# A gated two-branch layer: 128x128 transposes moved from TensorE to VectorE's square blocks and DMA

## The chip, the cores and the metric

The kernel runs on one core of one Trainium2 chip. The metric is the device time of one execution in microseconds (us). Of the kernel before, three runs were timed: 711.83, 712.28 and 712.83 us, median 712.28. One further execution was profiled; every duration below comes from it.

## The reference

One layer on x of 512 tokens and 1024 channels, in float32. A normalised x is projected to many columns at once; two token mixers take their parts, and their outputs are gated, projected and merged.

```
h    = rmsnorm(x) ;  proj = h @ w_in + b_in
mq, mk, mv, mi, mf, mo, mz, sq, sk, sv, sz, gates = split(proj)
# A) 4 memory heads of 256: causal conv and silu on mq, mk; chunkwise mLSTM with decay weights
hm   = rmsnorm(mlstm(mq, mk, mv, mi, mf))       per head
y_m  = hm * sigmoid(mo) * silu(mz)
# B) 8 attention heads of 128, "stick breaking", strictly causal
z    = (rmsnorm(q) @ rmsnorm(k).T) * scale
a    = sigmoid(z) * product over the keys between of (1 - sigmoid(z))
y_s  = (a @ v) * silu(sz)
out  = x + (sigmoid(g_m) * (y_m @ w_proj_m) + sigmoid(g_s) * (y_s @ w_proj_s)) @ w_out
```

## The kernel before, in words

**Precision.** A float32 product is made of three matmuls in a reduced format: each operand is split into a high part (ScalarE copies and rounds, L90) and a low part (VectorE subtracts, L91), and `mm3` (L85 to L87) adds high by high, high by low and low by high.

**Units.** The dense work is a list of 118 units, each with one 512 KB tile of weights. A unit is 24 matmuls of 512 columns in two halves. `chan_group` makes units whose result has channels on the partitions (one unit per 128 channels); `tok_group` makes units whose result has tokens on the partitions (four units for 512 channels, results all evicted at the end of the fourth). Units 0 to 31 are q, k, V and z (the gate) of attention set 0 and set 1, four heads in each; 32 to 71 belong to the two pairs of memory heads; 72 to 87 are the merge gates; then come the projections and the output.

**The main loop.** For each unit c the loop evicts the result of unit c-1, splits the weights of unit c+2 (AHEAD), issues the load of unit c+4 (LOADS), issues the unit's first half on TensorE, resumes every active head once, and issues the unit's second half. The heads are generators: at each `yield` a head stops until the next unit. So a head's small matmuls stand between dense matmuls, and a head takes as many units as it has yields. A head begins at or after its number in SB_START or M_START; in the units in REST no head is resumed. All engines work their instructions in the order in which the loop issued them. SyncE issues the loads in that order too, and it stands still at one whose buffer is not free or whose semaphore is still in use.

**An attention head** (`SbSet.head`). First step: q and k of the head are transposed on TensorE (L389) and split. Second: scores of query blocks 3, 0 and 1 on TensorE; `weigh` makes the weights of blocks 3 and 0 out of them (two sigmoids on ScalarE at L414 and L418, masks on GpSimd, a scan over the products at L422 and a product at L423 on VectorE). Third: the same for blocks 1 and 2. Now a_t[i], a part of the tile a_all (tag A, four buffers), holds weights with queries on the partitions; the product with V needs keys there. `turn` transposes the 128x128 blocks on TensorE by the identity (L447), into PSUM, and splits the result out of PSUM into at_split (tag P5, two buffers). `turn((0,))` and `turn((1,))` take 4 + 3 blocks in the fourth step, `turn((2, 3))` 2 + 1 blocks in the fifth, ten in all; `apply` multiplies with V in the fifth and sixth, and at L475 VectorE multiplies the gate y_s by the result. The fourth step waits until V of the set is complete.

**A memory head** (`MPair.head`). Row by row of key blocks `score` makes p_all (high and low, tag A); `num(i)` makes the output of token block i, VectorE and ScalarE normalise it into hns (L752, L755; tag P5). After the last one, eight 128x128 blocks are transposed on TensorE (L769) into PSUM, and VectorE multiplies y_m by them (L771).

Of the kernel before, what the change touches and what calls it, by code (L numbers as in the profile page):

```python
# [23 lines left out]

SB_START = [10, 13, 16, 20, 27, 30, 33, 36]
M_START = [52, 56, 70, 76]
GATES_PREP, GATES_START = 3, 4
REST = {11, 16, 20, 23, 24, 28, 44, 64}  # L30
AHEAD, LOADS = 2, 4


# [1 line left out]
def tile_hybrid_layer(  # L35
# [16 lines left out]
    nc = tc.nc  # L52
# [8 lines left out]
    sp = pool("sp")  # L61
# [19 lines left out]
    def att_ps():  # L81
        return psa.tile([128, 512], F32, name="aps", tag="aps")
# [6 lines left out]
    def split(src, hi, lo):  # L89
        nc.scalar.activation(hi, src, AF.Copy)  # L90
        nc.vector.tensor_tensor(lo, src, hi.bitcast(F32), op=OP.subtract)  # L91
# [119 lines left out]
    ident = cst.tile([128, 128], F32, name="ident")  # L211
# [97 lines left out]
    y_m = [None] * 8  # L309
    done = set()  # L310

    class SbSet:
# [70 lines left out]
        def head(self, h):  # L383
            hs = slice(h * 128, (h + 1) * 128)
            tr = []
            for name in ("q", "k"):
                tp = att_ps()
                for tb in range(TB):
                    nc.tensor.transpose(tp[:, tb * 128:(tb + 1) * 128], self.raw[name][tb][:, hs], ident)  # L389
                th = blk("qk", FR, name=name + "th")  # L390
                tl = blk("qk", FR, name=name + "tl")
                if name == "q":
                    nc.scalar.activation(th, tp, AF.Copy, scale=qkw)
                    nc.vector.scalar_tensor_tensor(tl, tp, qkw, th.bitcast(F32), op0=OP.mult, op1=OP.subtract)
                else:
                    split(tp, th, tl)
                tr.append((th, tl))
            yield
            (qh, ql), (kh, kl) = tr
            a_all = sp.tile([128, 1280], F32, name="a_all", tag="A", bufs=4)  # L400
            a_t = [a_all[:, 64 * i * (i + 1):64 * (i + 1) * (i + 2)] for i in range(TB)]

            def score(i, zp):
                n = (i + 1) * 128
                ts = slice(i * 128, n)
                mm3(zp, qh[:, ts], ql[:, ts], kh[:, 0:n], kl[:, 0:n], True, True)

            def weigh(i, zp):
                n = (i + 1) * 128
                ts = slice(i * 128, n)  # L410
                r, rn = self.r[i]
                om = blk("om", shape=(516,))
                be = a_t[i]
# [8 lines left out]
                nc.vector.tensor_tensor_scan(back, back, back, 1.0, op0=OP.mult, op1=OP.bypass)  # L422
                nc.vector.tensor_tensor(be, be, om[:, 1:n + 1], op=OP.mult)  # L423
# [7 lines left out]
            yield  # L431
            z2 = att_ps()
            score(2, z2[:, 0:384])
            weigh(1, z01[:, 128:384])
            weigh(2, z2[:, 0:384])
            yield
            while not ("v", self.s) in done:
                yield
            a_parts = {}

            def turn(js):
                tp = att_ps()
                at = 0
                for j in js:
                    n = T - j * 128
                    for i in range(j, TB):
                        nc.tensor.transpose(tp[:, at + (i - j) * 128:at + (i - j + 1) * 128],  # L447
                                            a_t[i][:, j * 128:(j + 1) * 128], ident)
                    at += n
                ap = blk("P5", FR, (2, 512), name="at_split")  # L450
                ah, al = ap[:, 0, :], ap[:, 1, :]
                split(tp[:, 0:at], ah[:, 0:at], al[:, 0:at])
                at = 0
                for j in js:
                    n = T - j * 128
                    a_parts[j] = ah[:, at:at + n], al[:, at:at + n]
                    at += n
# [140 lines left out]
    class MPair:  # L598
# [84 lines left out]
        def head(self, h):  # L683
            hd = 2 * self.p + h
# [50 lines left out]
            def num(i):  # L735
# [18 lines left out]
                nc.gpsimd.tensor_tensor(r, r, dn, op=OP.mult)  # L754
                return lambda: nc.scalar.activation(hn, sum_v, AF.Copy, scale=r)  # L755

            scale = [num(0), num(1)]
            for i in (2, 3):
                yield
                for fn in scale:  # L760
                    fn()
                scale = [num(i)]
            yield
            scale[0]()
            yield
            for d in range(2):
                tp = att_ps()
                for i in range(TB):
                    nc.tensor.transpose(tp[:, i * 128:(i + 1) * 128], hns[:, i, d * 128:(d + 1) * 128], ident)  # L769
                y = y_m[2 * hd + d]  # L770
                nc.vector.tensor_tensor(y, tp, y, op=OP.mult)  # L771


    sets = [SbSet(0), SbSet(1)]
# [4 lines left out]
    sets[0].z_group()  # L779
    sets[1].qk_group("q", C_SQ)  # L780
    sets[1].qk_group("k", C_SK)
    sets[1].v_group()
    sets[1].z_group()
    for p in pairs:
        p.o_group()
        p.z_group()
# [426 lines left out]
```

## Time and profile before

| | |
|---|---|
| median of three runs | 712.28 us (711.83 to 712.83) |
| profiled execution, its own time | 712.63 us |
| its span on the core | 710.9 us |
| TensorE busy | 702.3 us, 3332 matmuls |
| VectorE busy | 446.6 us, 711 instructions |
| ScalarE busy | 335.6 us, 629 instructions |
| GpSimd busy | 107.6 us, 249 instructions |
| mean granted TensorE clock | 0.999 |
| bytes moved by DMA | 73.57 MB, mean 103 GB/s |

The difference of 1.7 us between the execution's time and its span lies before the first and after the last instruction. In the profile PE is TensorE's matmuls, PEld its weight loads, DVE VectorE, ACT ScalarE, POOL GpSimd, SP SyncE; a q behind an engine's name stands for its sequencer, which waits and issues DMAs. L447 is line 447 of the kernel. A group's row ends in "busy us, mean ns | idle time before, and what ended it". A tile's name stands without its number, so that wl<-stg,wh reads: the low half wl is written from stg and wh. Matmuls overlap: a record of 390 ns for a 512-column matmul does not mean that they follow each other at that distance.

### The profile page before, as it was taken

To read this page: it belongs to the slowest core of one execution; us is meant where nothing else is said; L and a number is where in the kernel's file an instruction comes from. 1 tells how busy PE (TensorE), PEld (TensorE's weight loads), DVE (VectorE), ACT (ScalarE), POOL (GpSimd) and SP (SyncE) were. 2 spreads that over 40 slices of the span, in tenths; PEclk is the share of its full clock that TensorE was granted. 3 is DMA by queue.
4 is the path that set the end of the run, shared out by engine and by line. 5 is a ranking of instruction groups with operands and counts; after the bars stand their busy time and mean duration, and the time that the engine had idled before them with its cause. 6 is when DMAs were issued, how large, how long until landed. Compare 5 with 4: busy or idle time off the path is not lost.

```text
span 710.9 us, 9127 instructions
## 1 busy us (share of the span) xinstructions
PE 702.3 (99%) x3332; PEld 587.3 (83%) x3332; DVE 446.6 (63%) x711; ACT 335.6 (47%) x629; POOL 107.6 (15%) x249
## 2 busy tenths in 40 slices
PE   7999999999999999999999999999999999999997
PEld 5888888888888888888888888888888888888876
DVE  6837886656487567379954637885433244535896
ACT  6245364376355445144465634447464353334461
POOL 5412022253012112000011110000111000011010
PEclk9999999999999999999999999999999999999999
DMA  6433322232323223333332233333322236489434
GB/s 242 134 105 87 106 83 81 63 102 73 104 77 90 59 60 89 103 90 89 89 89 89 59 105 89 89 89 89 89 60 66 84 119 221 138 191 206 133 78 130
DMA packets 93492, 73.57 MB, mean 103 GB/s; under 512 B 3694, under 2 KB 77832, under 8 KB 93448
## 3 DMA queue, kind: packets, MB, share of 16 engines
q1 hardware_dynamic: 91288, 67.10, 32.6%
q0 software_dynamic: 2016, 5.77, 4.4%
q8 instruction: 26, 0.43, 0.2%
q14 instruction: 18, 0.15, 0.1%
q10 hardware_dynamic: 144, 0.13, 0.1%
HBM read 65.12 MB, written 2.10 MB: 95 GB/s over the span
## 4 chain that ended last, share of the span: by engine, by line
PE 97%; DMA 1%; DVE 1%; POOL 0%; SPq 0%; issue 0%; ACT 0%; DVEq 0%
PE dps L85 27%; PE dps L86 27%; PE dps L87 27%; PE aps L86 3%; PE aps L87 3%; PE aps L85 3%; PE aps L447 1%; PE aps L389 1%; PE dps L1102 1%; PE dps L1100 1%; PE dps L1101 1%; DMA stg<-in_w_in_dram 1%; PE aps L742 1%; PE aps L744 1%; PE aps L743 1%; PE aps L769 0%
## 5 line engine op out<-in xcount | busy, mean ns | idle before, releaser
L91 DVE TENSOR_TENSOR wl<-stg,wh 128x1024 fp32r<-128x1024 f32 x92 | 112.7, 1225 | 123.7 <-ACT wh L90 123.5
L85 PE MATMUL dps<-hh,wh 128*128 128x512 f32 x448 | 175.5, 392 | 0.0
L87 PE MATMUL dps<-hh,wl 128*128 128x512 f32 x448 | 174.8, 390 | 0.0
L86 PE MATMUL dps<-hl,wh 128*128 128x512 f32 x448 | 174.7, 390 | 0.0
L90 ACT ACTIVATE wh<-stg 128x1024 fp32r<-128x1024 f32 x92 | 96.8, 1052 | 63.3 <-PE dps L87 41.2
L87 PEld LDWEIGHTS dps<-hh,wl 128*128 128x128 f32 x448 | 84.2, 188 | 17.6
L85 PEld LDWEIGHTS dps<-hh,wh 128*128 128x128 f32 x448 | 84.2, 188 | 16.7
L86 PEld LDWEIGHTS dps<-hl,wh 128*128 128x128 f32 x448 | 84.2, 188 | 16.7
L85 PE MATMUL dps<-wh,hh 128*128 128x512 f32 x224 | 88.3, 394 | 0.0
L87 PE MATMUL dps<-wh,hl 128*128 128x512 f32 x224 | 87.4, 390 | 0.0
L86 PE MATMUL dps<-wl,hh 128*128 128x512 f32 x224 | 87.4, 390 | 0.0
L87 PEld LDWEIGHTS dps<-wh,hl 128*128 128x128 f32 x224 | 42.1, 188 | 8.9
L85 PEld LDWEIGHTS dps<-wh,hh 128*128 128x128 f32 x224 | 42.1, 188 | 8.2
L86 PEld LDWEIGHTS dps<-wl,hh 128*128 128x128 f32 x224 | 42.1, 188 | 8.2
L633 DVE SCALAR_TENSOR_TENSOR acc<-tmp,vec,acc 128x511 f32<-128x511 f32 (+2 forms) x48 | 36.0, 750 | 1.7
L636 ACT ACTIVATE tmp<-acc 128x512 f32<-128x512 f32 x16 | 10.1, 634 | 50.2 <-DVE acc L633 50.2
L416 POOL TENSOR_SCALAR_AFFINE_SELECT om<-om 128x128 f32<-128x128 f32 x32 | 12.1, 379 | 134.5 <-ACT om L414 134.5
L422 DVE TENSOR_TENSOR_SCAN om<-om 128x512 f32<-128x512 f32 (+3 forms) x32 | 27.9, 872 | 6.3 <-POOL om L416 6.3
L695 POOL TENSOR_SCALAR_AFFINE_SELECT w_all<-om 128x128 f32<-128x128 f32 x16 | 5.1, 355 | 167.1 <-DVE om L690 167.1
L90 ACT ACTIVATE at_split<-aps 128x384 fp32r<-128x384 f32 (+1 forms) x24 | 11.8, 525 | 36.8 <-PE aps L447 36.8
L91 DVE TENSOR_TENSOR at_split<-aps,at_split 128x384 fp32r<-128x384 f32 (+1 forms) x24 | 13.7, 599 | 19.8 <-ACT at_split L90 19.8
L85 PE MATMUL dps<-yh,wh 128*128 128x512 f32 x64 | 24.9, 389 | 0.0
(273 smaller groups left out, 1249.5 us busy)
## 6 DMA issues: line engine op xcount, KB each, us to landing
stg<-in_w_in_dram SPq DMA_DIRECT2D x87, 512.0 KB, 3.6
stg<-in_w_proj_s_dram SPq DMA_DIRECT2D x8, 512.0 KB, 4.0
B<-in_w_out_dram SPq DMA_DIRECT2D x8, 512.0 KB, 5.1
stg<-in_w_proj_m_dram SPq DMA_DIRECT2D x8, 512.0 KB, 3.6
wl<-stg POOLq DMA_DIRECT2D x8, 512.0 KB, 5.6
brow<-in_b_in_dram SPq DMA_DIRECT2D x8, 256.0 KB, 3.8
xr<-in_x_dram SPq DMA_DIRECT2D x8, 256.0 KB, 7.1
out_dram<-xr SPq DMA_DIRECT2D x7, 256.0 KB, 2.0
```

Of the source, the lines that this page charges most:

```text
L85: nc.tensor.matmul(ps, ah, bh, start=first, stop=False)
L86: nc.tensor.matmul(ps, ah, bl, start=False, stop=False)
L87: nc.tensor.matmul(ps, al, bh, start=False, stop=last)
L90: nc.scalar.activation(hi, src, AF.Copy)
L91: nc.vector.tensor_tensor(lo, src, hi.bitcast(F32), op=OP.subtract)
L389: nc.tensor.transpose(tp[:, tb * 128:(tb + 1) * 128], self.raw[name][tb][:, hs], ident)
L416: nc.gpsimd.affine_select(out=om[:, ts], in_=om[:, ts], compare_op=OP.is_gt, fill=1.0, base=0, channel_multiplier=1, pattern=[[-1, 128]])
L422: nc.vector.tensor_tensor_scan(back, back, back, 1.0, op0=OP.mult, op1=OP.bypass)
L447: nc.tensor.transpose(tp[:, at + (i - j) * 128:at + (i - j + 1) * 128], a_t[i][:, j * 128:(j + 1) * 128], ident)
L633: nc.vector.scalar_tensor_tensor(acc[:, j:], t[:, 0:T - j], cw(3 - j, ch), acc[:, j:], op0=OP.mult, op1=OP.add)
L636: nc.scalar.activation(t, acc, AF.Sigmoid)
L742: nc.tensor.matmul(nm[:, 0:258], ph, vh, start=j == 0, stop=False)
```

## The change

The transposes of L447 and L769 leave TensorE. VectorE's transpose turns each 32x32 square of a tile in its place, so that within each square rows and columns are exchanged, while the squares stay where they are. The exchange of the squares across partitions is made by DMAs from SBUF to SBUF, each of 32 partitions.

- Attention heads: `blocks(i)` turns the i+1 blocks of 128x128 of a_t[i] into a new tile ay (tag A, like a_all). Blocks 3 and 0 are turned in the third step, ahead of `weigh(1)` and `weigh(2)`; blocks 1 and 2 in a new step of their own. Then sixteen DMAs on SyncE's queue fill az (tag P5), eight in a step and eight in the next; one more step passes; then `turn` splits az, in SBUF, into ath and atl (tag y). A head has four more steps, and three fewer PSUM tiles.
- Memory heads: `turn(i)` turns hns of token block i into ht (tag A); turn(0) and turn(1) are issued ahead of num(3), turn(2) and turn(3) one and two steps later. Sixteen DMAs fill hz (tag A) in one step, and two steps later VectorE multiplies y_m by hz. A head has three more steps.
- SB_START begins the heads 3, 4, 5, 6 and 7 one, one, two, two and two units earlier; in REST 28 becomes 32; set 1's gate z comes ahead of its V.

```diff
-SB_START = [10, 13, 16, 20, 27, 30, 33, 36]
+SB_START = [10, 13, 16, 19, 26, 28, 31, 34]
-REST = {11, 16, 20, 23, 24, 28, 44, 64}
+REST = {11, 16, 20, 23, 24, 32, 44, 64}
...
+            ay = sp.tile([128, 4, 10, 32], F32, name="ay", tag="A", bufs=4)
+
+            def blocks(i):
+                for j in range(i + 1):
+                    nc.vector.transpose(ay[:, :, slot[i, j], :],
+                                        a_t[i][:, j * 128:(j + 1) * 128].rearrange("p (a j) -> p a j", j=32))
+
             z2 = att_ps()
             score(2, z2[:, 0:384])
+            blocks(3)
+            blocks(0)
             weigh(1, z01[:, 128:384])
             weigh(2, z2[:, 0:384])
+            yield
+            for i in (1, 2):
+                blocks(i)
+            yield
+            az = sp.tile([128, 4, 10, 32], F32, name="az", tag="P5", bufs=2)
+            for b in range(4):
+                for a in range(4):
+                    nc.sync.dma_start(az[32 * a:32 * a + 32, b, :, :], ay[32 * b:32 * b + 32, a, :, :])
+                if b == 1:
+                    yield
+            yield
             yield
             while not ("v", self.s) in done:
                 yield
...
             def turn(js):
-                tp = att_ps()
...
-                        nc.tensor.transpose(tp[:, at + (i - j) * 128:at + (i - j + 1) * 128],
-                                            a_t[i][:, j * 128:(j + 1) * 128], ident)
...
-                split(tp[:, 0:at], ah[:, 0:at], al[:, 0:at])
...
+                ah, al = blk("y", FR, name="ath"), blk("y", FR, name="atl")
+                split(az[:, :, n0:n1, :].rearrange("p b i j -> p i b j"),
+                      *[x[:, 0:at].rearrange("p (i b j) -> p i b j", b=4, j=32) for x in (ah, al)])
...
+            ht = sp.tile([128, 8, TB, 32], F32, name="ht", tag="A", bufs=4)
+
+            def turn(i):
+                nc.vector.transpose(ht[:, :, i, :], hns[:, i, :].rearrange("p (x j) -> p x j", j=32))
+
             scale = [num(0), num(1)]
             for i in (2, 3):
                 yield
                 for fn in scale:
                     fn()
+                if i == 3:
+                    turn(0)
+                    turn(1)
                 scale = [num(i)]
             yield
             scale[0]()
+            turn(2)
+            yield
+            turn(3)
+            yield
+            hz = sp.tile([128, 2, T], F32, name="hz", tag="A", bufs=4)
+            src = ht.rearrange("p (d a) i j -> p a d (i j)", d=2)
+            for a in range(4):
+                for b in range(4):
+                    nc.sync.dma_start(hz[32 * a:32 * a + 32, :, 128 * b:128 * b + 128],
+                                      src[32 * b:32 * b + 32, a])
+            yield
             yield
             for d in range(2):
-                tp = att_ps()
-                for i in range(TB):
-                    nc.tensor.transpose(tp[:, i * 128:(i + 1) * 128], hns[:, i, d * 128:(d + 1) * 128], ident)
-                y = y_m[2 * hd + d]
-                nc.vector.tensor_tensor(y, tp, y, op=OP.mult)
+                y = y_m[2 * hd + d].rearrange("p (i b j) -> p i b j", i=TB, b=4)
+                z = hz[:, d, :].rearrange("p (b i j) -> p i b j", i=TB, b=4)
+                nc.vector.tensor_tensor(y, z, y, op=OP.mult)
...
     sets[1].qk_group("k", C_SK)
+    sets[1].z_group()
     sets[1].v_group()
-    sets[1].z_group()
```

How the change moves instructions is shown at three places, in the order in which they stand on an engine, first before and then after. The first is TensorE in a unit in which one head applies its first weights and another computes scores (dps is dense work, aps a head's; at_split, then ath and atl, are the split weights, vh and vl V, kth and qth the split k and q). Before:

```order
L87 MATMUL dps<-hh,wl 128x512
L85 MATMUL aps<-at_split,vh 128x512
L86 MATMUL aps<-at_split,vh 128x512
L87 MATMUL aps<-at_split,vl 128x512
L85 MATMUL aps<-at_split,vh 128x384
L86 MATMUL aps<-at_split,vh 128x384
L87 MATMUL aps<-at_split,vl 128x384
L447 MATMUL aps<-ident,a_all 128x128 x3
L85 MATMUL aps<-kth,qth 128x384
L86 MATMUL aps<-ktl,qth 128x384
L87 MATMUL aps<-kth,qtl 128x384
```

After:

```order
L87 MATMUL dps<-wh,hl 128x512
L85 MATMUL aps<-ath,vh 128x512
L86 MATMUL aps<-atl,vh 128x512
L87 MATMUL aps<-ath,vl 128x512
L85 MATMUL aps<-ath,vh 128x384
L86 MATMUL aps<-atl,vh 128x384
L87 MATMUL aps<-ath,vl 128x384
L85 MATMUL aps<-kth,qth 128x512
L86 MATMUL aps<-ktl,qth 128x512
```

The product with V is followed at once by the scores of another head (here blocks 3, 0 and 1 instead of block 2, since the heads now stand otherwise to each other); no L447 stands between, there or anywhere else.

The second place is VectorE in the units 13 to 15, with heads 0 and 1 (SCALAR_TENSOR_TENSOR at L422 is the scan, wl the low half of weights two units ahead). Before:

```order
L325 SCALAR_TENSOR_TENSOR ys<-dps,bvec,tmp 128x512
L91 TENSOR_TENSOR wl<-stg,wh 128x1024
L422 SCALAR_TENSOR_TENSOR om<-om 128x256
L423 TENSOR_TENSOR a_all<-a_all,om 128x256
L422 SCALAR_TENSOR_TENSOR om<-om 128x384
L423 TENSOR_TENSOR a_all<-a_all,om 128x384
L394 SCALAR_TENSOR_TENSOR qtl<-aps,qkw,qth 128x512
L91 TENSOR_TENSOR ktl<-aps,kth 128x512
L325 SCALAR_TENSOR_TENSOR ys<-dps,bvec,tmp 128x512
L91 TENSOR_TENSOR wl<-stg,wh 128x1024
L91 TENSOR_TENSOR at_split<-aps,at_split 128x512
L91 TENSOR_TENSOR at_split<-aps,at_split 128x384
```

After:

```order
L91 TENSOR_TENSOR wl<-stg,wh 128x1024
L440 STREAM_TRANSPOSE ay<-a_all 128x4x32 x5
L422 SCALAR_TENSOR_TENSOR om<-om 128x256
L423 TENSOR_TENSOR a_all<-a_all,om 128x256
L422 SCALAR_TENSOR_TENSOR om<-om 128x384
L423 TENSOR_TENSOR a_all<-a_all,om 128x384
L394 SCALAR_TENSOR_TENSOR qtl<-aps,qkw,qth 128x512
L91 TENSOR_TENSOR ktl<-aps,kth 128x512
L325 SCALAR_TENSOR_TENSOR ys<-dps,bvec,tmp 128x512
L91 TENSOR_TENSOR wl<-stg,wh 128x1024
L440 STREAM_TRANSPOSE ay<-a_all 128x4x32 x5
L422 SCALAR_TENSOR_TENSOR om<-om 128x512
```

Two groups of five transposes come in, one ahead of the scans of blocks 1 and 2 and one in the next unit, and the splits of at_split move to a later unit.

The third place is SyncE's queue while the attention heads of set 0 and set 1 are at work (stg is a unit's weights, brow a bias row). Before:

```order
L304 DMA brow<-in_b_in_dram 128x512
L110 DMA stg<-in_w_in_dram 128x8x128 x2
L110 DMA stg<-in_w_in_dram 128x2x512 x6
L304 DMA brow<-in_b_in_dram 128x512
L110 DMA stg<-in_w_in_dram 128x2x512 x4
```

After:

```order
L110 DMA stg<-in_w_in_dram 128x2x512 x4
L458 DMA az<-ay 32x320 x8
L110 DMA stg<-in_w_in_dram 128x2x512 x2
L458 DMA az<-ay 32x320 x8
L304 DMA brow<-in_b_in_dram 128x512
L110 DMA stg<-in_w_in_dram 128x2x512
L458 DMA az<-ay 32x320 x8
L110 DMA stg<-in_w_in_dram 128x2x512
L458 DMA az<-ay 32x320 x8
```

Between the loads of the weights, which stood alone with the bias rows, now stand sixteen copies per head in two eights; the loads keep their order but for the swap of V and z.

More of the change, by code (lines that the diff above doesn't have):

```diff
@@ L431, in head @@
             yield
+            slot = {}
+            for j in range(TB):
+                for i in range(j, TB):
+                    slot[i, j] = len(slot)
+            ay = sp.tile([128, 4, 10, 32], F32, name="ay", tag="A", bufs=4)
[3 more added lines that the diff above has]
+                                        a_t[i][:, j * 128:(j + 1) * 128].rearrange("p (a j) -> p a j", j=32))
             z2 = att_ps()
             score(2, z2[:, 0:384])
+            blocks(3)
+            blocks(0)
             weigh(1, z01[:, 128:384])
             weigh(2, z2[:, 0:384])
+            yield
[9 more added lines that the diff above has]
+            yield
             yield
@@ L441, in turn @@
             def turn(js):
-                tp = att_ps()
-                at = 0
-                for j in js:
-                    n = T - j * 128
-                    for i in range(j, TB):
-                        nc.tensor.transpose(tp[:, at + (i - j) * 128:at + (i - j + 1) * 128],
-                                            a_t[i][:, j * 128:(j + 1) * 128], ident)
-                    at += n
-                ap = blk("P5", FR, (2, 512), name="at_split")
-                ah, al = ap[:, 0, :], ap[:, 1, :]
-                split(tp[:, 0:at], ah[:, 0:at], al[:, 0:at])
[L453 to L457, printed above, removed]
+                n0, n1 = slot[js[0], js[0]], slot[TB - 1, js[-1]] + 1
+                at = (n1 - n0) * 128
+                ah, al = blk("y", FR, name="ath"), blk("y", FR, name="atl")
+                split(az[:, :, n0:n1, :].rearrange("p b i j -> p i b j"),
+                      *[x[:, 0:at].rearrange("p (i b j) -> p i b j", b=4, j=32) for x in (ah, al)])
+                for j in js:
+                    o, n = (slot[j, j] - n0) * 128, T - j * 128
+                    a_parts[j] = ah[:, o:o + n], al[:, o:o + n]
             turn((0,))
```

## The prediction, made before the changed kernel was run

> **What bounds the kernel now.** I read the page first, then who waits on TensorE, then the chain, then one unit of the timeline.
>
> ```profile
> span 710.9 us, 9127 instructions
> ...
> PE 702.3 (99%) x3332; PEld 587.3 (83%) x3332; DVE 446.6 (63%) x711; ACT 335.6 (47%) x629; POOL 107.6 (15%) x249
> ...
> PEclk9999999999999999999999999999999999999999
> ...
> PE 97%; DMA 1%; DVE 1%; POOL 0%; SPq 0%; issue 0%; ACT 0%; DVEq 0%
> ```
>
> TensorE is busy for 99% of the span, at the full granted clock, and the chain that ended last is 97% TensorE. A busy share can hide gaps, so the next view is what TensorE waited for, all of it:
>
> ```profile
> PE dps L1078 <- DVE idle L1073: 1.5, 1, 1.5
> PE aps L293 <- DVE x L283: 1.2, 1, 1.2
> PE dps L1100 <- DVE hh L295: 0.9, 1, 0.9
> PE dps L1102 <- DVE fl L1059: 0.7, 1, 0.7
> ```
>
> Four waits, 4.3 us, and all four lines belong to the start (warming, first x tiles, first weights). From the first projection on, TensorE never waits. So any TensorE time that is taken out is gained one for one, as long as no new wait appears; and work that is added to another engine costs nothing until it makes TensorE wait.
>
> **What is removed from TensorE.** The transposes of the attention weights (L447) and of the memory heads' outputs (L769):
>
> ```profile
> L447 PE MATMUL aps<-ident,a_all 128*128 128x128 f32 x80 | 11.4, 273 | 0.0
> ...
> L769 PE MATMUL aps<-ident,hns 128*128 128x128 f32 x32 | 4.1, 272 | 0.0
> ```
>
> 80 and 32 of them. The 273 ns is the length of one record, and records overlap in the pipeline, so it is not the price. The price is what the chain gives a run of them (start, length):
>
> ```profile
> 103.82 0.77 PE aps L447 x7
> ...
> 112.62 0.33 PE aps L447 x3
> ...
> 415.62 0.87 PE aps L769 x8
> ```
>
> 0.77/7, 0.33/3 and 0.87/8 are all 0.11 us each. A second reading checks this. One unit of the projection is 24 matmuls of 512 columns; the unit between 254.90 and 262.00 also holds seven L447 and eight L389, which are the same kind of transpose:
>
> ```profile
> 254.90 0.39 PE L85 MATMUL dps<-hh,wh 128*128 128x512 f32 x1
> 255.13 0.39 PE L86 MATMUL dps<-hl,wh 128*128 128x512 f32 x1
> ...
> 257.62 0.93 PE L447 MATMUL aps<-ident,a_all 128*128 128x128 f32 x7
> ...
> 258.39 0.60 PE L389 MATMUL aps<-ident,qraw 128*128 128x128 f32 x4
> ...
> 259.18 0.48 PE L85 MATMUL dps<-hh,wh 128*128 128x512 f32 x1
> ...
> 262.00 0.39 PE L85 MATMUL dps<-hh,wh 128*128 128x512 f32 x1
> ```
>
> 262.00 - 254.90 = 7.10 us. Matmuls start every 0.23 us (255.13 - 254.90; 0.2275 over longer runs), 24 of them 5.46 us; 1.64 us is left for 15 transposes, 0.109 us each. So 112 x 0.11 = 12.3 us leave TensorE. The lower bound takes only start to start, 257.62 to 259.18 for 15: 0.104 each, 11.6 us. I take 12.3, since the unit as a whole, with what follows the run, was longer by 0.109 each. An upper bound adds the 13 waits at L447:
>
> ```profile
> L447 PEldq EVENT_SEMAPHORE  x13: 51/51/51, 99.6 to 275.7; - x13
> ```
>
> 13 x 0.051 = 0.7 us, 13.0 in all.
>
> The Trainium skill, "VectorE: DVE Perf Modes", section "The three transpose paths", gives TensorE 390 ns for a 128x128 transpose (bf16); 112 of those would be 43.7 us, an estimate by that page. The trace disagrees for this kernel: 0.11 us on the chain, so the page's figure is not used.
>
> **What is added to VectorE.** Per attention head ten transposes of 128x128 in five-and-five, per memory head four of 128x256. The trace has no such instruction. The nearest rows are SBUF to SBUF in float32:
>
> ```profile
> L355 DVE TENSOR_SCALAR kraw<-kraw,rk 128x128 f32<-128x128 f32 x32 | 6.5, 272 | 0.0
> ...
> L423 DVE TENSOR_TENSOR a_all<-a_all,om 128x256 f32<-128x256 f32 x8 | 3.9, 485 | 0.9
> ...
> L422 DVE TENSOR_TENSOR_SCAN om<-om 128x128 f32<-128x128 f32 x8 | 4.0, 505 | 0.0
> ```
>
> One input, one output, 128 columns: 0.272 us; the slowest instruction of that width, the scan: 0.505. So 2.7 to 5.1 us per attention head, 22 to 40 over eight; memory heads 4 x 0.485 = 1.9 us each, up to twice that. I take the low ends, because a transpose has one input like L355. Whether this fits is read from the stage, not from the average:
>
> ```profile
> 97.00:295.00 198.00, 198.00 (x997) 168.34 (x996) 127.45 (x182) 98.17 (x207) 43.30 (x113) 1.00 0.29 81
> ...
> 232.00:254.90 22.90, 22.90 (x122) 19.67 (x120) 14.04 (x20) 11.01 (x19) 4.26 (x12) 1.00 0.26 70
> ...
> 379.00:442.00 63.00, 63.00 (x326) 54.05 (x326) 34.07 (x64) 30.20 (x59) 8.89 (x32) 1.00 0.29 80
> ```
>
> Columns: stretch, its length, busy TensorE, weight loads, VectorE, ScalarE, GpSimd. In the stage of the attention heads VectorE works 127 of 198 us. One head's period (232.00 to 254.90, three units) has 14.0 of 22.9; after the change the period is 1.1 us shorter, and 14.0 + 2.7 = 16.7, or 19.1 at the scan's price, still fits into 21.8. In the memory heads' stage there is more room, 34 of 63. The splits of the weights stay, three per head on ScalarE and VectorE, of the same sizes; they now read SBUF instead of PSUM, and I cost that at nothing within the same room.
>
> What is queued behind the transposes on VectorE is the low half wl of the weights two units ahead. Its slack:
>
> ```profile
> 255.10 0.69 ACT L608 ACTIVATE ym<-dps,bvec 128x512 f32<-128x512 f32 x1 [1.71 <-PE dps L87]
> ...
> 262.20 0.69 ACT L618 ACTIVATE tmp<-dps,bvec 128x512 f32<-128x512 f32 x1 [1.90 <-PE dps L87]
> ...
> 270.60 0.69 ACT L618 ACTIVATE tmp<-dps,bvec 128x512 f32<-128x512 f32 x1 [1.61 <-PE dps L87]
> ```
>
> ```profile
> 256.77 1.22 DVE L91 TENSOR_TENSOR wl<-stg,wh 128x1024 fp32r<-128x1024 f32 x1 [1.55 <-ACT wh L90]
> ```
>
> The evictions mark the ends of units. wl is done at 257.99 for the unit that begins about 270.4: a lead of 12 us. VectorE may fall that far behind once before TensorE notices.
>
> **What is added to SyncE and the DMAs.** Sixteen copies of 32 partitions per head (40 KB each for attention, 32 KB for memory heads), in the queue of the weight loads. The attention heads' go out eight in one step and eight in the next; the memory heads' go out sixteen at once.
>
> ```profile
> L110 SPq DMA_DIRECT2D stg<-in_w_in_dram x87: 367/368/464, 2.1 to 549.3; - x87
> ```
>
> ```profile
> stg<-in_w_in_dram SPq DMA_DIRECT2D x87, 512.0 KB, 3.6
> ...
> b_rows<-in_b_in_dram SPq DMA_DIRECT2D x2, 8.0 KB, 1.6
> ```
>
> An issue costs SyncE 0.37 us, so eight cost 2.9; landing lies between 1.6 (8 KB) and 3.6 us (512 KB): 6.5 us at most, inside one step of about 7.1. The split that reads them stands two steps after the second eight are issued, 14.2 us, so some 7.7 us are spare before ScalarE would stand and wait, and then the lead above. A memory head's sixteen take 5.9 + 3.6 = 9.5 us, and their reader on VectorE stands two steps of at least 5.46 us later, 1.4 us to spare and then the lead. Behind the copies on SyncE wait the weight loads of the next step:
>
> ```profile
> 258.02 0.37 SPq L110 DMA_DIRECT2D stg<-in_w_in_dram  x1
> ```
>
> ```profile
> 271.19 1.05 ACT L90 ACTIVATE wh<-stg 128x1024 fp32r<-128x1024 f32 x1
> ```
>
> Loads run four units ahead and splits two, so the load issued at 258.02 is split at 271.19: 13.2 us, of which its landing takes 3.6. Being 6 us late behind eight copies, it still comes in time; cost 0, and only beyond 9.6 us would ScalarE wait.
>
> **Moves.** The begins of five heads move by one or two units, the second gate's four units go before those of its V, with their loads, the bias row and their evictions. The matmuls are the same and TensorE's queue stays full, so they cost 0; the cover is the lead above. Set 1's V is complete four units later than before, at unit 32; head 4 begins at 26, has four more steps than before and asks for V at step 34, so it doesn't wait. The last memory head begins at 76 as before and ends at step 87, three units later than before and seven before its output is split. The new square tile ht shares four buffers with two heads' p_all, so its first transpose on VectorE waits for the matmuls of its head's num(3); these stand in the middle of the same unit, so at most half a unit, about 3 us, four times, again under the lead.
>
> **Sum.** Profiled execution 712.63 - 12.3 = 700.3 us. That execution was 0.35 us above the median of the runs (712.28), so 700.0 for the median. A measurement of this kernel can tell about 0.2%, 1.4 us, from no change.
>
> **Rivals.**
>
> *A, VectorE falls behind in places.* At 1.0 us per transpose (four passes of 0.272) a head's period has 14.0 + 10 = 24.0 us of work in 21.8; eight heads pile up 18 us, the lead takes 12 to 13, and about 5 us of waiting eat into the gain: 705. It decides from 0.78 us per transpose, (21.8 - 14.0)/10. For it: the trace shows no transpose at all, and the moved begins put some heads beside the evictions of z. Against: even the scan is at 0.505. At 1.1 us or a little more the gain is gone: no change.
>
> *B, slower: SyncE's small copies hold up the weight loads.* SyncE has seen small DMAs crawl once:
>
> ```profile
> 6.48 6.44 SPq L208 DMA_DIRECT2D v_rows<-in_conv_w_dram  x4
> ...
> 15.51 1.20 SPq L208 DMA_DIRECT2D b_rows<-in_b_in_dram  x3
> ```
>
> Four issues took 6.44 us, 1.61 each, because each waited for an earlier DMA to land. If all go at 2.0 us (a landing of a store of 256 KB)
>
> ```profile
> out_dram<-xr SPq DMA_DIRECT2D x7, 256.0 KB, 2.0
> ```
>
> sixteen and three loads are 33.1 us of SyncE per head, 265 for eight, where 24 steps between the first and last begin and three more are 27 x 7.2 = 194 us, and 12.6 us of lead; TensorE waits 58 us: 758. It decides near 1.64 us per copy, where 219 us are 12.3 over 207. Against: at the start the queue was full of 512 KB loads, and the three issues at 15.51 took 0.4 each with several in flight. A rule of the Trainium skill speaks for B, "DMA: Bandwidth & Descriptors", section "Bandwidth": transfers under 64 KB are dominated by their descriptors. The only copy from SBUF to SBUF in the trace is a large one of another queue:
>
> ```profile
> xr<-u POOLq DMA_DIRECT2D x6, 256.0 KB, 3.7
> ```
>
> It lands in 3.7 us and says nothing of many small ones, so the trace does not settle this rule.
>
> That the change does not do what it says is ruled out by the order of the instructions: no L447 or L769 is left on TensorE.
>
> **Chances.** All hidden, 700.0: 0.72. A with a partial loss, 701.5 to 706: 0.18. A at a price that takes the gain: 0.03. B: 0.07. Hence faster 0.90, same 0.03, slower 0.07. The range: its low end is 712.28 - 13.0 - 0.45 (the fastest run before lies 0.45 under the median) = 698.8; its high end takes the lower bound of the gain (712.28 - 11.6 = 700.7) and goes on through A to 705.5, which leaves out the rest of A and B, about 0.12.
>
> **What would show it.** Right: TensorE waits for nothing new after 35 us, its instructions fall by 112 to 3220, the span is near 698.5, the new transposes take 0.25 to 0.5 us, and the copies land within 4 us. A: transposes above 0.8 us, VectorE near full between 100 and 290 us, TensorE waiting for wl. B: SyncE's issues above 1.6 us, loads of stg late, ScalarE waiting for az or stg. The forecast is wrong if the span is above 703 us, or if TensorE waits for over 3 us past the start.

## The result, and the profile after

The changed kernel took 700.60 us (median of 4 runs, 700.42 to 700.79), beside 712.17 for the kernel before (4 runs, 711.83 to 712.83): ratio 0.9836, 95% interval 0.9819 to 0.9853. The forecast was 700.0, with a range of 698.8 to 705.5. The profiled execution took 700.42 us, and the one of before 712.63.

The page after, its span, busy times and chain:

```profile
span 698.7 us, 9267 instructions
...
PE 690.4 (99%) x3220; PEld 575.2 (82%) x3220; DVE 463.5 (66%) x807; ACT 335.6 (48%) x629; POOL 109.2 (16%) x249
...
PE 97%; DMA 1%; DVE 1%; POOL 0%; SPq 0%; issue 0%; ACT 0%; DVEq 0%
```

The span is 12.2 us shorter, TensorE has 112 matmuls fewer and is busy 11.9 us less, VectorE has 96 instructions and 16.9 us more, ScalarE is as it was. TensorE still carries 97% of the chain. All that it waited for:

```profile
PE dps L1115 <- DVE idle L1110: 1.5, 1, 1.5
PE aps L293 <- DVE x L283: 1.0, 1, 1.0
PE dps L1137 <- DVE hh L295: 0.9, 1, 0.9
PE dps L1139 <- DVE fl L1096: 0.7, 1, 0.7
```

These are the same four waits of the start as before (the lines have other numbers, the tiles the same names). This view lists no other, so what was taken out of TensorE came out of the time. The new work, in the groups by shape:

```profile
L440 DVE STREAM_TRANSPOSE ay<-a_all 128x128 f32<-128x128 f32 x80 | 17.2, 275 | 0.0
...
L91 DVE TENSOR_TENSOR atl<-az,ath 128x384 fp32r<-128x384 f32 x16 | 9.1, 570 | 1.8 <-PE aps L86 1.4 <-ACT ath L90 0.3
L780 DVE STREAM_TRANSPOSE ht<-hns 128x256 f32<-128x256 f32 x16 | 6.6, 430 | 3.1 <-PE aps L761 3.1
...
L808 DVE TENSOR_TENSOR ym<-hz,ym 128x512 f32<-128x512 f32 x8 | 5.1, 683 | 0.0
```

The record of a 128x128 transpose on VectorE is 0.275 us long, that of a 128x256 one 0.430. In a run of five (1.08 us, below) the next starts 0.20 us after the one before: these records overlap as TensorE's do. The memory heads' transposes waited 3.1 us in all for num(3) on TensorE (the tile that ht shares). The copies on SyncE, by their line: the first row's times are the issues in ns (least, median, most), then the first and the last start; the second row is from issue to landing in us:

```profile
L458 SPq DMA_DIRECT2D az<-ay x128: 507/588/1646, 104.8 to 271.9; - x128
...
DMA to landing us min/median/max: 1.8/2.0/6.5
```

```profile
129.15 0.37 SPq L110 DMA_DIRECT2D stg<-in_w_in_dram  x1
129.57 5.49 SPq L458 DMA_DIRECT2D az<-ay  x8
```

One copy keeps SyncE for 0.59 us, against 0.37 for a load of 512 KB, and eight in a row take 5.49, 0.69 each. That still fits into a unit of some 7 us. The stages, in the same columns as in the prediction:

```profile
97.00:290.00 193.00, 192.94 (x928) 162.35 (x927) 139.45 (x261) 99.25 (x208) 43.67 (x110) 1.00 0.41 113
...
379.00:442.00 63.00, 63.00 (x311) 53.58 (x310) 38.14 (x69) 31.62 (x61) 7.76 (x28) 1.00 0.34 92
```

VectorE works 139 of 193 us with the attention heads (127 of 198 before), 38 of 63 with the memory heads. TensorE misses 0.06 us in the 193.

That 0.06 us is worth a look. It stands where VectorE evicts the result of a group with tokens on the partitions (q of set 1, L335), which frees the PSUM that the next unit needs. VectorE after:

```profile
136.11 1.08 DVE L440 STREAM_TRANSPOSE ay<-a_all 128x128 f32<-128x128 f32 x5
...
137.74 0.68 DVE L91 TENSOR_TENSOR ktl<-aps,kth 128x512 fp32r<-128x512 f32 x1
138.34 0.68 DVE L335 TENSOR_TENSOR qraw<-dps,brow 128x512 f32<-128x512 f32 x1
```

and TensorE after:

```profile
138.71 0.39 PE L87 MATMUL dps<-wh,hl 128*128 128x512 f32 x1
139.16 0.47 PE L85 MATMUL dps<-wh,hh 128*128 128x512 f32 x1
```

The first eviction ends at 139.02, and the next unit's first matmul follows 0.14 us later, 0.45 after the start of the one ahead of it, where 0.23 is usual. In the kernel before, the same eviction and the first matmul of the next unit were

```profile
143.95 0.68 DVE L335 TENSOR_TENSOR qraw<-dps,brow 128x512 f32<-128x512 f32 x1
```

```profile
145.14 0.39 PE L85 MATMUL dps<-wh,hh 128*128 128x512 f32 x1
```

0.51 us from the end of the one to the start of the other, of which 0.14 to 0.15 stay even where TensorE stands and waits for an eviction of this line (dve_x2 and dma_x2, below). Ahead of the eviction in the queue now stand five transposes and the splits of another head's q and k (the ktl row is the last of them), where before stood the splits of at_split. They have used up the margin and, by the starts, 0.22 us more. The forecast had not looked there. Four of the experiments did.

### The profile page after: what moved, and what is told of

Read it like the earlier page. It is cut to its first block, busy times and chain, and to the rows that moved or that the text cites. A ratio compares the mean times of both kernels' runs of the same rounds, so it can differ in the third digit from the quotient of the medians.

```text
span 698.7 us, 9267 instructions
## 1 busy us (share of the span) xinstructions
PE 690.4 (99%) x3220; PEld 575.2 (82%) x3220; DVE 463.5 (66%) x807; ACT 335.6 (48%) x629; POOL 109.2 (16%) x249
## 4 chain that ended last, share of the span: by engine, by line
PE 97%; DMA 1%; DVE 1%; POOL 0%; SPq 0%; issue 0%; ACT 0%; DVEq 0%
PE dps L85 27%; PE dps L86 27%; PE dps L87 27%; PE aps L86 3%; PE aps L87 3%; PE aps L85 3%; PE aps L389 1%; PE dps L1139 1%; PE dps L1137 1%; PE dps L1138 1%; DMA stg<-in_w_in_dram 1%; PE aps L760 1%; PE aps L762 1%; PE aps L761 1%; DVE fl L1096 0%; POOL fl L1096 0%
## 5 line engine op out<-in xcount | busy, mean ns | idle before, releaser
L86 PEld LDWEIGHTS dps<-hl,wh 128*128 128x128 f32 x448 | 84.2, 188 | 16.9
L654 ACT ACTIVATE tmp<-acc 128x512 f32<-128x512 f32 x16 | 10.1, 633 | 50.8 <-DVE acc L651 50.8
L422 DVE TENSOR_TENSOR_SCAN om<-om 128x512 f32<-128x512 f32 (+3 forms) x32 | 26.7, 835 | 8.8 <-POOL om L416 8.8
L416 POOL TENSOR_SCALAR_AFFINE_SELECT om<-om 128x128 f32<-128x128 f32 x32 | 14.1, 441 | 109.0 <-ACT om L414 109.0
L414 ACT ACTIVATE om<-aps,rq 128x512 f32<-128x512 f32 (+3 forms) x32 | 16.8, 525 | 22.8 <-PE aps L87 22.8
L86 PE MATMUL dps<-yl,wh 128*128 128x512 f32 x64 | 24.9, 389 | 0.0
```

The source lines that it names most:

```text
L86: nc.tensor.matmul(ps, ah, bl, start=False, stop=False)
L654: nc.scalar.activation(t, acc, AF.Sigmoid)
```

## Experiments

Each kernel ran beside the kernel before on the same chip. That kernel took 712.19 us beside sb_only, m_only, swap_rest and dve_x2, 712.15 beside a_oldrest, dve_off, dma_x2 and dma_x4, and 712.00 beside the other four. The change was not run again; "above the change" is above its 700.60 us. No experiment leaves out any of the computation; where transposes are repeated, the later ones write the same values again. The moved begins without the rest of the change were not tried.

**The two parts apart.** sb_only is the change with the memory heads as before (the turns, copies and extra steps taken out, L769's transposes put back):

```diff
-                if i == 3:
-                    turn(0)
-                    turn(1)
...
-            turn(2)
-            yield
-            turn(3)
-            yield
-            hz = sp.tile([128, 2, T], F32, name="hz", tag="A", bufs=4)
...
+                for i in range(TB):
+                    nc.tensor.transpose(tp[:, i * 128:(i + 1) * 128], hns[:, i, d * 128:(d + 1) * 128], ident)
```

m_only is the kernel before with just these lines the other way round.

> The attention heads' part alone, with its begins and the gate ahead of V; the memory heads transpose on TensorE as before. If the gain is the time of the transposes on TensorE and nothing else, 32 of the 112 come back at 0.11 us each: 700.6 + 3.5 = 704.1 us, 8.0 under the kernel before. If the gain came with the moved begins and the gate and not with the transposes, this kernel keeps it all: 700.6.

> The memory heads' part alone. By the transposes' own time: 712.2 - 32 x 0.11 = 708.7 us. If the wait of VectorE for num(3) or the sixteen copies at once cost TensorE something, less than 3.5 us are gained; if nothing is gained, 712.2.

sb_only took 704.38 us (703.75 to 704.90; ratio 0.9891, 0.9877 to 0.9904), m_only 708.80 (708.72 to 708.90; ratio 0.9953, 0.9941 to 0.9966). That is 7.8 us for 80 transposes, 0.098 each, and 3.4 us for 32, 0.106 each; together 11.2 of the 11.6 of the whole. Each part pays with the time of its own transposes on TensorE, and neither needs the other.

**The second gate ahead of its V, without the rest.** swap_rest is the kernel before with two of the moves, swap_only has the last three lines alone:

```diff
-REST = {11, 16, 20, 23, 24, 28, 44, 64}
+REST = {11, 16, 20, 23, 24, 32, 44, 64}
...
-    sets[1].v_group()
     sets[1].z_group()
+    sets[1].v_group()
```

> The kernel before with set 1's gate ahead of its V and with unit 32 instead of 28 as a rest: moves without any change of the transposes. If TensorE's list of work alone sets the time, 712.2 us, no change beyond 1 us either way. If the moves bring part of the 11.6 us, that part shows here.

> The kernel before with set 1's gate ahead of its V and nothing else (rest in unit 28 as before). If the heads of set 1, which have four steps fewer here, pile up at the wait for V and then want VectorE and TensorE at once, it is slower like the run that also moved the rest: 716 to 720. If that loss came with the moved rest, 712.2.

swap_rest took 718.94 us (ratio 1.0096, 1.0080 to 1.0111), swap_only 718.06 (ratio 1.0082, 1.0068 to 1.0096): 6 to 7 us slower than before; in swap_only it is the order of two groups of four units alone that costs 6. New waits of TensorE in swap_only:

```profile
PE aps L85 <- ACT a_all L418: 1.4, 1, 1.4
PE dps L85 <- DVE tmp L372: 1.3, 1, 1.3
...
PE aps L85 <- DVE at_split L91: 1.2, 1, 1.2
...
PE aps L389 <- DVE at_split L91: 0.4, 1, 0.4
```

4.3 us between 224 and 251 us; the profiled execution was 5.1 us longer than that of before. The second of these rows, on VectorE and on TensorE:

```profile
223.79 0.29 DVE L423 TENSOR_TENSOR a_all<-a_all,om 128x128 f32<-128x128 f32 x1
224.00 1.28 DVE L372 TENSOR_TENSOR tmp<-dps,brow 128x512 f32<-128x512 f32 x2
```

```profile
224.74 0.50 PE L85 MATMUL dps<-hh,wh 128*128 128x512 f32 x1 [1.30 <-DVE tmp L372]
```

V's eviction (L372) now stands right behind a head's product with its scan (L423), and the next unit waits for it. The matmuls are the same and TensorE is still 98% busy: the order of units alone moves an eviction behind other work. The other three waits, 3.0 us, are for a head's own products and were not followed further. In the changed kernel the same order brings no wait. That kernel has longer heads, other begins and no transposes of the weights in PSUM; which of these repairs it was not told apart.

**REST as before, in the changed kernel.** a_oldrest:

```diff
-REST = {11, 16, 20, 23, 24, 32, 44, 64}
+REST = {11, 16, 20, 23, 24, 28, 44, 64}
```

> The changed kernel with unit 28 as a rest again and not unit 32, in which V of set 1 is evicted. If the place decides, the heads' work of unit 32 and the one before now stands around V's four evictions, and TensorE waits there: 1 to 4 us, 702 to 705. If the moves only matter through TensorE's own list, which is as long as before, 700.6.

701.21 us (701.05 to 701.55; ratio 0.9844, 0.9832 to 0.9857): 0.6 above the change, and one new wait, 0.6 us at V's eviction L372 (221.0 us). The place and the size of the wait fit together, but 0.6 us is less than can be told from no change.

**VectorE's transposes twice.** dve_x2 turns each block of the attention heads twice, in a stage where VectorE has 54 us free. By the length of the records that is 80 x 0.27 = 22 us more. Since they overlap, VectorE is busy for 14.0 us more (463.5 to 477.5 over the whole span):

```diff
-                for j in range(i + 1):
-                    nc.vector.transpose(ay[:, :, slot[i, j], :],
-                                        a_t[i][:, j * 128:(j + 1) * 128].rearrange("p (a j) -> p a j", j=32))
+                for _ in range(2):
+                    for j in range(i + 1):
+                        nc.vector.transpose(ay[:, :, slot[i, j], :],
+                                            a_t[i][:, j * 128:(j + 1) * 128].rearrange("p (a j) -> p a j", j=32))
```

> The changed kernel with every block of the attention weights turned twice on VectorE (the second time over the first): 80 more transposes of 0.27 us, 21.5 us more work. The prediction's sum says that VectorE makes TensorE wait only from 0.78 us per block; here it is 0.54, so 700.6 us. If the cover is already used up (one head's period has 18.8 of 22.9 us busy, and 21.5 with this), TensorE waits, and several us are lost: 703 to 710.

702.53 us (702.40 to 702.80; ratio 0.9866, 0.9852 to 0.9879), 1.9 above the change. Two new waits of TensorE, both for an eviction:

```profile
PE dps L85 <- DVE qraw L335: 1.0, 1, 1.0
PE dps L85 <- DVE tmp L372: 0.9, 1, 0.9
```

The first, on VectorE and on TensorE:

```profile
135.97 2.04 DVE L441 STREAM_TRANSPOSE ay<-a_all 128x128 f32<-128x128 f32 x10
...
138.56 0.68 DVE L91 TENSOR_TENSOR ktl<-aps,kth 128x512 fp32r<-128x512 f32 x1
139.16 0.67 DVE L335 TENSOR_TENSOR qraw<-dps,brow 128x512 f32<-128x512 f32 x1
```

```profile
139.98 0.47 PE L85 MATMUL dps<-wh,hh 128*128 128x512 f32 x1 [1.03 <-DVE qraw L335]
```

Ten transposes in place of five move the eviction from 138.34 to 139.16 and the matmul behind it from 139.16 to 139.98, 0.82 us each. TensorE waits for no wl. So it isn't the room in a period that ends first, but the little room ahead of an eviction in its unit.

**The extra transposes put elsewhere.** If only the place counts, extra work in other heads must be free. dve_off turns the blocks of heads 0, 1, 4, 6 and 7 three times (100 more; VectorE is busy 18.1 us longer than in the change) and those of 2, 3 and 5 once; dve_x2_off turns those of all heads but 2 and 5 twice (60 more; 10.2 us longer):

```diff
-                for j in range(i + 1):
+                for j in list(range(i + 1)) * (1 if 4 * self.s + h in (2, 3, 5) else 3):
```

```diff
-                for j in range(i + 1):
+                for j in list(range(i + 1)) * (1 if 4 * self.s + h in (2, 5) else 2):
```

> The changed kernel with the blocks of heads 0, 1, 4, 6 and 7 turned three times on VectorE, those of heads 2, 3 and 5 once: 100 more transposes of 0.27 us, 26.9 us more work, a quarter more than in the run that turned every block twice, but none of it in the two units ahead of the evictions of set 1's q, k and V. If the place decides (TensorE waits only where those evictions, at L335 and L372, free the banks of PSUM for the next unit), 700.6 us. If the sum of VectorE's work decides, the loss grows with it: 1.9 x 26.9 / 21.5 = 2.4 us, 703.0.

> The changed kernel with every block of heads 0, 1, 3, 4, 6 and 7 turned twice on VectorE, those of heads 2 and 5 once: 60 more transposes, 16 us, five more in a unit at most (1.35 us). The run with all blocks turned twice waited 1.9 us, at two places alone, the evictions of set 1's q and V, behind the blocks of heads 2 and 5. If what decides is what VectorE owes TensorE within the same or the next unit, both waits go: 700.6 us. If the sum of VectorE's work decides, three quarters of the loss stay: 1.9 x 60 / 80 = 1.4 us, 702.0.

dve_off took 703.62 us (703.17 to 704.01; ratio 0.9877, 0.9864 to 0.9890), dve_x2_off 700.72 (700.55 to 701.79; ratio 0.9842, 0.9828 to 0.9855). New in dve_off:

```profile
PE aps L86 <- DVE ktl L91: 1.3, 3, 0.8
...
PE dps L85 <- DVE ys L325: 0.6, 1, 0.6
```

dve_x2_off has none, and it is the change in time. By the times alone, a sum that is free up to some 10 us and costs from there would do as well: 10.2 us more cost nothing, 14.0 cost 1.9 us and 18.1 cost 3.0. It is the traces that speak for the place. In dve_x2 the doubled blocks of six heads brought no wait, and both waits went when those of heads 2 and 5 were turned once. But the theory that only the evictions of q, k and V are such places fell with dve_off: there TensorE waits three times for ktl, the low half of k that the head's scores need in its next unit, and once for the eviction of a gate (L325). Other products that TensorE takes from VectorE within the same unit or the next are such places too, and at 20 transposes more in a head they come up. These waits add up to 1.9 us of the 3.0; the rest was not traced.

**The memory heads' transposes four times.** m_x4, 48 x 0.43 = 21 us more:

```diff
             def turn(i):
-                nc.vector.transpose(ht[:, :, i, :], hns[:, i, :].rearrange("p (x j) -> p x j", j=32))
+                for _ in range(4):
+                    nc.vector.transpose(ht[:, :, i, :], hns[:, i, :].rearrange("p (x j) -> p x j", j=32))
```

> The changed kernel with each of the memory heads' sixteen transposes made four times: 48 more of 0.43 us, 20.6 us more of VectorE's work, as much as in the run that turned every attention block twice, but in a stage where VectorE works 38 of 63 us. If room within a unit decides, 700.6 us, at most 1 us more where turn(0) and turn(1) stand in one unit with 2.6 us more. If any work of VectorE costs at the rate of that run, 702.5.

702.07 us (701.93 to 702.26; ratio 0.9858, 0.9844 to 0.9871), 1.5 above the change. By the time alone this can't be told well from a loss by the sum (702.5 was expected for that). The trace has one new wait, again for an eviction, of V in the memory heads' stage, where VectorE still has 17 of 63 us free:

```profile
421.82 1.88 DVE L781 STREAM_TRANSPOSE ht<-hns 128x256 f32<-128x256 f32 x4
423.62 1.25 DVE L688 TENSOR_TENSOR tmp<-dps,brow 128x512 f32<-128x512 f32 x2
```

```profile
PE dps L85 <- DVE tmp L688: 1.3, 1, 1.3
```

```profile
379.00:442.00 63.00, 61.73 (x304) 52.24 (x303) 46.30 (x90) 29.28 (x57) 10.86 (x27) 1.00 0.32 90
```

**More copies.** dma_x2 cuts every copy of the attention heads in two (32 a head), dma_x4 in four (64 a head); the bytes stay:

```diff
-                    nc.sync.dma_start(az[32 * a:32 * a + 32, b, :, :], ay[32 * b:32 * b + 32, a, :, :])
+                    for lo, up in ((0, 5), (5, 10)):
+                        nc.sync.dma_start(az[32 * a:32 * a + 32, b, lo:up, :], ay[32 * b:32 * b + 32, a, lo:up, :])
```

> The changed kernel with every copy of the attention heads cut into two of 20 KB: 32 copies per head on SyncE. At the measured 0.59 us each 18.9 us, with three loads 20.5 of a head's period of 21.8: SyncE just keeps up, 700.6 us. If small copies hold up the loads at once (rival B), TensorE waits for stg by way of ScalarE: over 702.

> The same cut into four of 8 to 12 KB: 64 copies per head, 37.7 us on SyncE at 0.59 each, 39.4 with three loads, 315 for eight heads against 207 us (194 us of steps and the lead of 12.6). By rival B's sum TensorE waits about 108 us: 809. If cut copies issue faster (0.3 us or less), SyncE keeps up, and it is 700.6.

dma_x2 took 715.78 us (713.19 to 717.21; ratio 1.0045, 1.0031 to 1.0060): 15 above the change, and its whole gain gone. dma_x4 took 872.80 (872.52 to 873.43; ratio 1.2255, 1.2238 to 1.2273). The copies of dma_x2 by their line, and one stretch of SyncE:

```profile
L459 SPq DMA_DIRECT2D az<-ay x256: 507/589/1535, 104.6 to 297.4; - x128
...
DMA to landing us min/median/max: 1.7/1.8/4.8
```

```profile
152.19 11.08 SPq L459 DMA_DIRECT2D az<-ay  x16
163.32 0.58 SPq L304 DMA_DIRECT2D brow<-in_b_in_dram  x1
```

A copy of 20 KB takes SyncE as long as one of 40 KB did, 0.59 us and 0.69 from start to start, and lands in 1.8 us, against 2.0. Sixteen take 11.1 us in a unit of 7.1, and the bias row of k's eviction is queued behind them:

```profile
167.52 2.48 DVE L335 TENSOR_TENSOR kraw<-dps,brow 128x512 f32<-128x512 f32 x4 [3.47 <-DMA brow<-in_b_in_dram]
```

TensorE waits 3.1 us for this eviction. And the queue falls behind from head to head: the last copy goes out at 297.4 in place of 271.9, so ScalarE stands for the weights and then for the copies,

```profile
291.68 1.06 ACT L90 ACTIVATE wh<-stg 128x1024 fp32r<-128x1024 f32 x1 [9.59 <-DMA stg<-in_w_in_dram]
298.84 1.09 ACT L90 ACTIVATE ath<-az 128x512 fp32r<-128x512 f32 x2 [6.11 <-DMA az<-ay]
```

and TensorE for it:

```profile
PE aps L85 <- ACT ath L90: 7.0, 1, 7.0
PE dps L85 <- DVE kraw L335: 3.1, 1, 3.1
```

These 10.1 us are most of the 12.8 that this profiled execution (713.19) was longer than that of the change; about 1.9 more come from a lower clock behind the long wait (last section). It was also the shortest of its six runs, so the other 2.6 of the median are not in a trace. In dma_x4 the same two rows read 85.9 us (6 times) and 30.6. So rival B's loss exists, at more copies than the change has: the bytes are the same, and what counts is the number of issues.

**Without the bare step.** no_spare takes out the `yield` between the second eight copies and the split:

```diff
                 if b == 1:
                     yield
             yield
-            yield
             while not ("v", self.s) in done:
```

> The changed kernel without the step that passes between the second eight copies and the split of az. Eight copies take about 5.5 us on SyncE and land 2.0 us later, 7.5 us, where one unit has about 7: ScalarE waits half a microsecond or so per head, and the heads of set 1 come to V one unit earlier. If that stays covered, 700.6 us; if a late copy stops TensorE as in the run with cut copies, 702 or more.

699.89 us (699.67 to 701.23; ratio 0.9827, 0.9813 to 0.9840). This can't be told from the change (700.60), and TensorE waits only at the start. The step isn't needed; no version beat the change.

## Why the prediction was right, point by point

**The time taken from TensorE: right.** 112 transposes at 0.11 us were to be 12.3 us, between 11.6 and 13.0. By the medians of that comparison it was 11.6 (0.103 each), by the profiled executions 12.2 (0.109 each). The record of 273 ns would have given 31 us. The time that a run takes in the chain, and the rest of a unit after its dense matmuls, were the price; the length of a record in a pipelined engine was not.

**VectorE's new work: right by its records.** Foreseen 0.272 us a block from the nearest row with one input; measured 0.275. The memory heads' were taken at 0.485 and took 0.430. These are lengths of records, though. VectorE's time for a block in a run is 0.20 us, so this term was too high, by the same mistake that the prediction avoided on TensorE.

**That VectorE's work is hidden: right, but for a reason that does not hold.** The step that failed is the lead of wl, 12 us, by which "VectorE may fall that far behind once before TensorE notices". In none of the runs, not even in dma_x4, was wl what TensorE waited for. Where VectorE had more to do, TensorE waited for what VectorE owes it within the unit or the next, above all the eviction that frees PSUM: 0.51 us of distance at q's eviction before the change, 0.14 after it. That the change as it stands loses only 0.2 us there was luck, as far as the forecast goes. The prediction read slack from one product in the queue, not from the one that was due first. So rival A's threshold of 0.78 us per block was too high as well: at two records a block, 0.55 (dve_x2), TensorE already waits 1.9 us, though by A's sum 14.0 + 5.5 us fit into 21.8. A's chance was for a real loss, but it grows from the margins of single evictions and not from the sum over a period, which gave none here.

**SyncE's copies: hidden as foreseen, with less room than foreseen.** The issue was priced at 0.37 us and took 0.59, 0.69 in a row; eight are 5.5 us in place of 2.9. The landing, 2.0 us in the middle, lay inside its bounds; the longest, 6.5, did not, nor inside the 4 us that were named as a sign, and it cost nothing. The row from which B took its crawl was misread. By its line

```profile
L208 SPq DMA_DIRECT2D v_rows<-in_conv_w_dram x4: 418/422/5049, 6.5 to 12.5; - x4
```

one of the four issues kept SyncE for 5.05 us and the other three for 0.42, not 1.61 each. What held the one the trace does not show; the two waits of this line for an earlier DMA, 1.2 us in all, come after these four. Nor was xr<-u the only copy within SBUF: wl<-stg (512 KB, 5.6 us) is another, large as well.

Rival B's point was put at 1.64 us per copy; dma_x2, at 2 x 0.69 = 1.38 us per original copy, already loses more than the gain. B's sum allowed SyncE 194 us from the first begin to three units past the last. But in the changed kernel the copies run from 104.8 to 271.9 us, 167; with the lead of 12.6 that is 180. Sixteen at 1.38 and three loads of 0.37, eight times, are 185.5: 6 us too much, where the trace has 7.0 at that place. At 4 x 0.69 = 2.76 it is 362 - 180 = 182 us, 883 in all, and dma_x4 measured 872.8. So by this estimate, made after the runs, B decides near 1.4, and a wait inside a unit (the bias row) comes on top. The step of B's sum that failed is, by this estimate, the length of the stretch.

The prediction said that the trace did not settle a rule of the Trainium skill ("DMA: Bandwidth & Descriptors", "Bandwidth": under 64 KB a transfer is dominated by its descriptors). These runs agree with it as far as a time can that hardly falls with the size: 40 KB land in 2.0 us and 20 KB in 1.8. But the landing was hidden, and the price that decided, SyncE's time per issue, is not in the rule.

**Moves: cost 0 in the whole, not each by itself.** "The matmuls are the same and TensorE's queue stays full, so they cost 0" failed as a reason: swap_only, the same matmuls, lost 6 us. In the whole the moves cost nothing that can be told: the change is as fast as its transposes make it.

A rule that spoke against the change stands in the Trainium skill, "VectorE: DVE Perf Modes", "Rules for kernel authors": a 128x128 transpose belongs on TensorE where a result in PSUM will do. Before, it did do, and taking it off gained 11.6 us. Where TensorE carries 97% of the chain, 0.11 us there is dearer than a record of 0.275 us on VectorE and a share of sixteen copies.

## What to carry to other kernels

Where one engine is busy for 99%, price work that leaves it by what it adds to the chain, not by the length of its records (which misleads on the engine that takes it up as well), and let the other engines pay more, so long as they stay hidden. Whether they do is read from the margin of every product that the bound engine takes from them in the same unit or the next (first of all evictions that free PSUM), not from idle shares or from the product with the longest lead. With many small DMAs count the issues on the queue that also feeds the weights, unit by unit and over the real stretch from the first to the last.

## What the runs showed of the hardware that was not expected

SyncE is kept longer by a copy of 32 partitions within SBUF, 0.59 us (0.69 from start to start), than by a load of 512 KB (0.37), and halving the copy to 20 KB changes nothing in it. VectorE's records of 128x128 transposes overlap: 0.275 us long, they start every 0.20 us in a run.

After a wait of TensorE the granted clock fell. In dma_x2 TensorE stood for 7.0 us until 299.53; three stretches of that kernel, in the columns above:

```profile
289.00:296.50 7.50, 3.56 (x16) 2.63 (x14) 1.82 (x2) 1.06 (x1) 0.00 (x0) 1.00 0.31 98
296.50:303.30 6.80, 3.77 (x9) 2.95 (x10) 1.16 (x2) 2.16 (x4) 0.20 (x2) 0.50 0.65 183
303.30:310.00 6.70, 6.70 (x33) 5.62 (x33) 3.84 (x5) 1.47 (x2) 0.10 (x1) 1.00 0.73 196
```

The clock is 0.50 from 296.5, some 4 us into the wait, to 303.3, 3.8 us after its end; at half the pace the 3.8 us behind the wait cost about 1.9 us more. The wait of 3.1 us at 168 us left the clock at 1.00. In dma_x4, with many long waits, the mean over the execution was 0.907, and in one stretch:

```profile
400.00:460.00 60.00, 16.80 (x62) 13.15 (x63) 8.56 (x11) 5.59 (x9) 0.00 (x0) 0.61 0.14 35
```

So here the wait of 7.0 us cost more than itself, and the one of 3.1 us did not.
